# Hybrid encoder block on one core: the second MLP product's right operands on VectorE beside the first product, and three edges in the queues

## The chip, the cores and the metric

One core of a Trainium2 chip runs one layer of a streaming encoder (2048 positions, width 1024, MLP width 4096, all float32). The metric is the device time of one execution in microseconds (us), as the median of several runs. A profile is one execution recorded by the hardware: each engine's instructions with their times. Engines are called as the profile calls them: PE (TensorE, matmuls; PEld its weight loads), DVE (VectorE), ACT (ScalarE), POOL (GpSimd) and SP (SyncE, which only issues DMAs). Each engine works through its own instructions in order.

## The reference, cut to what matters

```python
mod = silu(c) @ w_ada + b_ada           # shift1, scale1, gate1, shift2, scale2, gate2
h = rms_norm(x, g_pre_mix) * (1 + scale1) + shift1
xin, b_gate, c_gate, q, k, v, g = split(h @ w_in)
y_conv = b_gate * causal_depthwise_conv3(c_gate * xin)
y_ret  = silu(g) * per_head_rms(retention(rotary(q), rotary(k), v))
x = x + gate1 * rms_norm(concat(y_conv, y_ret) @ w_out, g_post_mix)
h = rms_norm(x, g_pre_mlp) * (1 + scale2) + shift2
f = square(relu(h @ w_fc1)) @ w_fc2
x = x + gate2 * rms_norm(f, g_post_mlp)
```

## The kernel before, in words

**Precision.** Each float32 operand is split into a high part (an ACT cast to fp32r, `whi`, `wh`, `qh`, `fh`) and a low part (a DVE subtraction, `wlo`, `wl`, `ql`, `fl`). A product takes three matmuls: high by high, high by low, low by high (`mm3`, L142 to L144).

**The mixer** is a loop over four blocks `b` of 512 positions. Each block projects v, k, g, q, xin, the conv gate and the output gate in turn, does retention in four tiles, then the output product and a residual. Weights stream through three buffers (`wgroup`: load `raw` L134, cast L136, low part L138). `rotary` turns q and k out of PSUM with DVE (L541, L550) and a POOL add. `mod2` forms one modulation vector with eight DVE operations of 128x1024 (L429, L431), each on its own load `ada`; it is traced after the g projection in blocks 0 to 2, and once more in block 0.

**The MLP** works on two blocks `B` of 1024 positions, and each of its two products is done by a fast scheme with seven products of half size in place of eight (numbered 1 to 7; operands are sums and differences of quadrants). `fc1(B)` loops over 16 steps `t` of the MLP width. In each it makes sums of the weight quadrants on POOL (L901 to L904), does seven products `prod(i)` in the order 1, 2, 6, 7, 5, 3, 4 (at `t` = 0 of the first block, 4 comes before 7), squares, and stores the seven left operands of the second product to DRAM (`fd`). One product is 12 matmuls of 128x512. `fc2(B)` then runs seven products over 16 steps, each step loading a left operand (`fd`) and a right operand.

**The right operands of the second product.** Products 1, 2 and 3 use quadrants of the weight `w2` as they are. Those of 5, 7, 6 and 4 are differences, made once by `w2_prep(t)` for the 16 `t`: two loads of 512 KB (`w2r`), four POOL subtractions (L513), four stores to `w2d` (L515). `w2_some(n)` does `n` of them at set places of the mixer.

**The left operands** of block 0 (`h_left`) are split as 28 pieces before `fc1(0)`; three groups of four (for products 7, 5 and 3) are parked in DRAM (`sd`) and split during `t` = 0, where `left` is run to its end.

**Work beside fc1.** `fc1` takes a generator `beside` and calls `next` on it between products (`step`). For `fc1(0)` it is `mixer_end`: the residual of the mixer's last block (DVE L750, POOL L753, ACT squares L754) and then `h2_prep`, which transposes that block on PE (L492) for the second MLP block. For `fc1(1)` it is the tail of `fc2(0)`.

**Buffers.** The tag `x` has three buffers of 128x1024, shared by `x_tile`'s users: mod loads `ada`, residual loads `x`, `w2r` and, in fc2, `fw`. Weight halves `wh` and `wl` have three each, tag `r` ten; the `g` PSUM banks are six. `q(n, tag)` takes a 128x512 buffer from one of two pools by the parity of `n`.

**Order.** The program is traced in the order of the code, and a planner puts each engine's instructions in order from the traced order, the dependences and its own model of durations. So an instruction may go ahead of one that was traced earlier. `with tc.issue_after(ins)` adds an edge: what is traced inside on the engine of `ins` stays behind `ins` in that engine's order. It makes no engine wait on another.

Of the kernel before, what the change touches and what calls it, by code (L numbers as in the profile page):

```python
# [11 lines left out]
F32 = mybir.dt.float32  # L12
# [3 lines left out]
ALU = mybir.AluOpType  # L16
# [38 lines left out]
def block_kernel(  # L55
# [29 lines left out]
    def x_tile(name):  # L85
        return late.tile([P, D], F32, tag="x", name=nm(name), bufs=3)
# [417 lines left out]
    NP = DFF // P // 2  # L504
    w2d = {i: [dram.tile([P, 512], F32, name=f"w2d{i}_{t}") for t in range(NP)] for i in (5, 6, 7, 4)}

    def w2_prep(t):
        halves = [x_tile("w2r") for _ in range(2)]
        for i, c in enumerate(halves):
            nc.sync.dma_start(c, w2[t][:, i * 1024 : i * 1024 + 1024])  # L510
        c11, c12, c21, c22 = (c[:, i : i + 512] for c in halves for i in (0, 512))
        for o, a, b_ in ((c11, c12, c11), (c12, c22, c12), (c22, c22, c11), (c21, c21, c22)):
            nc.gpsimd.tensor_tensor(o, a, b_, op=ALU.subtract)  # L513
        for i, a in ((5, c11), (7, c12), (6, c22), (4, c21)):
            nc.sync.dma_start(w2d[i][t], a)  # L515

    w2_todo = iter(range(NP))

    def w2_some(n):
        for _, t in zip(range(n), w2_todo):  # L520
            w2_prep(t)

# [1 line left out]
    with pa_stack:  # L526
# [11 lines left out]
        def rotary(ps, coss, sins, t, dst):  # L538
            pv = ps.rearrange("p (h s d) -> p h s d", h=H, s=2)
            qa = tmp()  # L540
            nc.vector.tensor_tensor(  # L541
                qa.rearrange("p (x d) -> p x d", d=HALF),
                ps.rearrange("p (x d) -> p x d", d=HALF),
                coss[:, t, :].unsqueeze(1).to_broadcast([P, 2 * H, HALF]),
                op=ALU.mult,
            )
            qb = tmp()
            qbv = qb.rearrange("p (h s d) -> p h s d", h=H, s=2)
            for s in range(2):
                nc.vector.tensor_tensor(  # L550
                    qbv[:, :, s, :], pv[:, :, 1 - s, :],
                    sins[:, t, s, :].unsqueeze(1).to_broadcast([P, H, HALF]),
                    op=ALU.mult,
                )
            nc.gpsimd.tensor_tensor(dst, qa, qb, op=ALU.add)

        for b in range(NB):

# [5 lines left out]
            for ps in vps:  # L564
                v_ = at("va")
                nc.scalar.copy(v_, ps)
                vs.append(v_)
            if b > 0:
                w2_some(2)
            coss, sins = rope_tables(b)  # L570
            kds = []

            def k_end(t, ps):
                kr = tmp()
                rotary(ps, coss, sins, t, kr)
                kd = at("vb")
                nc.gpsimd.tensor_tensor(
                    kd.rearrange("p (h d) -> p h d", h=H),
                    kr.rearrange("p (h d) -> p h d", h=H),
                    kdec.unsqueeze(2).to_broadcast([P, H, DH]),  # L580
                    op=ALU.mult,
                )
                kds.append(kd)

            if b == 0:
                for t in range(3):
                    k_end(t, kps[t])
                k_end(3, gemm_nat(w_in(KK), h_cur, KS, ALL[3:])[0])
            else:
                for t, ps in enumerate(gemm_nat(w_in(KK), h_cur, KS)):  # L590
                    k_end(t, ps)

            sgs = []
            for ps in gemm_nat(w_in(GG), h_cur, KS):
# [1 line left out]
                nc.scalar.activation(sg, ps, AF.Silu)  # L596
                sgs.append(sg)
            if b < 3:
                part = mod2((0, 2, 3)[b])
            kTs = []  # L600
            for t in range(NT):
                tps = mbank()
# [102 lines left out]
            if b > 0:  # L705
                for _ in h2_prep(b - 1, h2_load(b - 1)):
                    pass
            w2_some(2 if b > 0 else 1)
            for j, ps in enumerate(gemm_t(w_in(BG), h_cur)):
                y = tmp()  # L710
                nc.vector.tensor_tensor(y, ps, cc[j], op=ALU.mult)
# [11 lines left out]
            for ch, tag in enumerate(("kT", "sg")):  # L723
                ms = []
                for t, ps in enumerate(gemm_nat([wout[ch * 4 + k0 // 2] for k0, _ in ko], ys, ko)):
                    m = at(tag)
                    nc.scalar.copy(m, ps)
                    nc.scalar.activation(junk(), m, AF.Square, accum_out=ssm[:, t, ch : ch + 1])
                    ms.append(m)
                mixs.append(ms)  # L730
                if ch == 0:
                    if b < NB - 1:
                        w2_some(1)

                    if b + 1 < NB:
                        rb = spread(r1)
                        h_cur = [h1_tile(b + 1, k, rb) for k in range(NK)]
# [77 lines left out]
    def split512(src, tile_of):  # L815
        hi, lo = tile_of("h"), tile_of("l")
        nc.scalar.copy(hi, src)  # L817
        nc.vector.tensor_tensor(lo, src, hi.bitcast(F32), op=SUB)  # L818
        return hi, lo

    def w_(part):
        return h_("w" + part)
# [62 lines left out]
    def fc1(B, hl, first, left=None, beside=None):  # L885
        def relu2(c, src):
            nc.scalar.activation(c, src, AF.Relu)
            nc.scalar.activation(c, c, AF.Square)

        def step(n=1):  # L890
            for _ in range(n if beside is not None else 0):
                next(beside, None)

        for t in range(NP):
            b11, b12, b21, b22 = first if t == 0 else quads(t)
            right = {}

            def prod(i):
                if i == 6:
                    t2 = r_()  # L900
                    nc.gpsimd.tensor_tensor(b11, b12, b11, op=SUB)  # L901
                    nc.gpsimd.tensor_tensor(t2, b22, b11, op=SUB)
                    nc.gpsimd.tensor_tensor(b12, b22, b12, op=SUB)
                    nc.gpsimd.tensor_tensor(b21, b21, t2, op=SUB)  # L904
                    right[6] = t2
                src = {1: b11, 2: b21, 7: b12, 5: b11, 3: b22, 4: b21}.get(i)
                hi, lo = split512(right[6] if i == 6 else src, w_)
                ps = bank()
                for p in range(4):
                    c = slice(p * P, p * P + P)  # L910
                    xh, xl = hl[i][p]
                    mm3(ps, hi[:, c], lo[:, c], xh, xl, p == 0, p == 3)
                return ps

            if t == 1 and left is not None:

                f12, f11, f21 = q(0, "junk"), q(0, "junk"), q(0, "sg")
            else:
                f12, f11, f21 = q(t, "kT"), q(t, "kT"), q(t, "kT")
            nc.scalar.copy(f12, prod(1))  # L920
            step()
            add(f11, prod(2), f12)
            step()
            relu2(f11, f11)
            nc.sync.dma_start(fd[B][1][t], f11)
            add(f12, prod(6), f12)
            step()
            f22 = q(t, "kT")
            if t == 0 and left is not None:
                nc.scalar.copy(f21, prod(4))  # L930
                for _ in left:
                    pass
                add(f22, prod(7), f12)
                add(f21, f21, f22, nc.gpsimd)
                beside_ = beside
                next(beside_, None)
                ps = prod(5)
                add(f12, ps, f12)
                add(f22, ps, f22)
                next(beside_, None)  # L940
            else:
                add(f21, prod(7), f12)
                step()
                ps = prod(5)
                add(f12, ps, f12)
                add(f22, ps, f21)
                step()
            relu2(f22, f22)
            nc.sync.dma_start(fd[B][4][t], f22)
            add(f12, prod(3), f12)  # L950
            relu2(f12, f12)
            nc.sync.dma_start(fd[B][2][t], f12)
            if t > 0 or left is None:
                add(f21, prod(4), f21)
            relu2(f21, f21)
            if beside is not None:
                for _ in beside:
                    pass
                beside = None

            s3 = q(t, "sg")
            nc.vector.tensor_tensor(s3, f11, f21, op=SUB)
            nc.sync.dma_start(fd[B][7][t], s3)
            nc.vector.tensor_tensor(f21, f21, f22, op=ADD)
            nc.sync.dma_start(fd[B][5][t], f21)
            s2_ = q(t, "sg")
            nc.vector.tensor_tensor(s2_, f21, f11, op=SUB)
            nc.sync.dma_start(fd[B][6][t], s2_)
            s4 = q(t, "sg")
            nc.vector.tensor_tensor(s4, f12, s2_, op=SUB)  # L970
            nc.sync.dma_start(fd[B][3][t], s4)

# [121 lines left out]
    left = h_left(0, hl[0], nc.vector, lambda n: r_(), False)  # L1094
    for _ in range(LEFT):
        next(left)
    fc1(0, hl[0], quads(0), left, mixer_end())
    tail = fc2(0, h_left(1, hl[1], nc.vector, lambda n: q(1, "kT" if n < 4 else "sg"), True))
    fc1(1, hl[1], quads(0), None, tail)
    fc2(1)  # L1100
# [84 lines left out]
```

## Time and profile before

| | |
|---|---|
| median of 3 runs | 2220.07 us (2219.22 to 2229.08) |
| profiled execution | 2219.7 us; span of its instructions 2217.9 us |
| mean granted TensorE clock | 0.994 |
| DMA | 428.22 MB, mean 193 GB/s |
| first matmul of fc1(0) / fc2(0) | 959.50 us / 1284.95 us |
| w2r loads issued | 174.5 to 807.5 us |

Busy time of an engine is the union of its instructions' times. Matmuls overlap in the pipeline, so each shows 0.39 us while the next starts after less; the distance of starts is what counts. "Idle before, releaser" names what the instruction had waited for last. A wait on an engine that is not the bound costs nothing by itself.

### The profile page before, as it was taken

Reading aid. Unit: us, or ns where it says so; the run is one execution under the profiler, and the core shown is the slowest. Engines: PE = TensorE matmul, PEld = TensorE weight load, DVE = VectorE, ACT = ScalarE, POOL = GpSimd, SP = SyncE. Lnnn points to the kernel's source line nnn. Section 1 sums busy time; section 2 is a strip of 40 time slices with the busy share of each in tenths; the row PEclk is TensorE's granted clock in tenths of the full one; section 3 lists DMA queues with packets and bytes.
Section 4 is the critical chain, followed back from the end, with each engine's and each line's share of the span. In section 5 each row is a group of like instructions: output and inputs, shape, how many; then the busy total and the mean of one; then the engine's idle time right before and its main releaser. Section 6 shows DMA issues by size and latency. Waiting matters only on the chain.

```text
span 2217.9 us, 28512 instructions
## 1 busy us (share of the span) xinstructions
PE 2143.4 (97%) x9784; PEld 1770.0 (80%) x9784; DVE 1435.4 (65%) x2186; ACT 995.5 (45%) x1730; POOL 559.2 (25%) x426
## 2 busy tenths in 40 slices
PE   6999999999999999989999999999999999999997
PEld 5787877877877888868888888888888888888885
DVE  8656863765577544776666787556766666555566
ACT  4423523253234422565555555445455555454453
POOL 0215164205332452152333301001333333010012
PEclk9999999999999999999999999999999999999998
DMA  8456477446555563665444376666764443666656
GB/s 342 133 172 224 139 261 240 147 156 228 190 199 188 189 234 97 231 204 196 157 157 157 129 250 215 200 191 190 273 210 157 157 156 123 209 191 195 196 189 251
DMA packets 197426, 428.22 MB, mean 193 GB/s; under 512 B 22561, under 2 KB 22561, under 8 KB 197281
## 3 DMA queue, kind: packets, MB, share of 16 engines
q1 hardware_dynamic: 197280, 426.41, 58.0%
q8 instruction: 76, 1.25, 0.2%
q14 instruction: 70, 0.57, 0.1%
HBM read 322.51 MB, written 103.81 MB: 192 GB/s over the span
## 4 chain that ended last, share of the span: by engine, by line
PE 70%; issue 11%; DMA 9%; DVE 4%; POOL 4%; ACT 1%; SPq 1%; DVEq 0%; POOLq 0%; ACTq 0%
PE g L142 20%; PE g L144 20%; PE g L143 20%; DMA w2r<-in_w 2%; PE m L142 2%; PE m L143 2%; PE m L144 2%; POOL w2r L513 2%; DMA w2d<-w2r 2%; DMA x<-in_x 1%; DMA ada<-in_ada 1%; DMA q<-h2d 1%; DVE wl L818 1%; DVE ql L818 1%; POOL sg L753 1%
## 5 line engine op out<-in xcount | busy, mean ns | idle before, releaser
L143 PE MATMUL g<-ql,wh 128*128 128x512 f32 x896 | 350.3, 391 | 8.7 <-DVE ql L818 8.7
L142 PE MATMUL g<-qh,wh 128*128 128x512 f32 x896 | 349.9, 391 | 1.4 <-ACT wh L817 1.1
L144 PE MATMUL g<-qh,wl 128*128 128x512 f32 x896 | 350.2, 391 | 0.1
L136 ACT CAST whi<-raw 128x1024 fp32r<-128x1024 f32 x148 | 155.6, 1052 | 338.7 <-PE g L144 186.0
L138 DVE TENSOR_TENSOR wlo<-raw,whi 128x1024 fp32r<-128x1024 f32 x148 | 200.5, 1360 | 159.0 <-ACT whi L136 157.9
L883 DVE TENSOR_TENSOR q<-g,q 128x512 f32<-128x512 f32 x267 | 178.4, 687 | 174.6 <-PE g L144 174.5
L143 PE MATMUL g<-wl,fh 128*128 128x512 f32 x680 | 264.9, 390 | 0.0
L144 PE MATMUL g<-wh,fl 128*128 128x512 f32 x680 | 264.6, 389 | 0.0
L818 DVE TENSOR_TENSOR fl<-fw,fh 128x512 fp32r<-128x512 f32 x218 | 161.4, 741 | 153.0 <-ACT fh L817 149.9
L817 ACT CAST wh<-r 128x512 fp32r<-128x512 f32 x224 | 138.9, 621 | 216.4 <-PE g L143 193.4
L817 ACT CAST fh<-fw 128x512 fp32r<-128x512 f32 x218 | 135.4, 621 | 214.9 <-DMA fw<-fd 201.3
L142 PE MATMUL g<-wh,fh 128*128 128x512 f32 x680 | 218.4, 389 | 0.9 <-ACT wh L817 0.9
L143 PEld LDWEIGHTS g<-ql,wh 128*128 128x128 f32 x896 | 168.9, 188 | 45.1 <-DVE ql L818 10.1
L142 PEld LDWEIGHTS g<-qh,wh 128*128 128x128 f32 x896 | 168.8, 188 | 37.4 <-ACT wh L817 1.8
L144 PEld LDWEIGHTS g<-qh,wl 128*128 128x128 f32 x896 | 168.9, 188 | 36.1 <-DVE wl L818 1.5
L818 DVE TENSOR_TENSOR wl<-fw,wh 128x512 fp32r<-128x512 f32 x218 | 156.6, 719 | 51.6 <-ACT wh L817 51.3
L1016 POOL TENSOR_TENSOR q<-q,gg 128x512 f32<-128x512 f32 x28 | 43.8, 1588 | 530.9 <-ACT q L1013 281.1
L818 DVE TENSOR_TENSOR wl<-r,wh 128x512 fp32r<-128x512 f32 x224 | 166.3, 743 | 9.8 <-ACT wh L817 9.5
L817 ACT CAST wh<-fw 128x512 fp32r<-128x512 f32 x218 | 135.2, 620 | 73.8 <-PE g L144 33.9
L901 POOL TENSOR_TENSOR r<-r,r 128x512 f32<-128x512 f32 x32 | 41.7, 1304 | 430.3 <-DVE wl L818 382.5
L142 PEld LDWEIGHTS g<-wh,fh 128*128 128x128 f32 x680 | 127.5, 188 | 28.2 <-ACT wh L817 1.7
L143 PEld LDWEIGHTS g<-wl,fh 128*128 128x128 f32 x680 | 127.7, 188 | 27.7 <-DVE wl L818 1.2
(258 smaller groups left out, 4412.5 us busy)
## 6 DMA issues: line engine op xcount, KB each, us to landing
raw<-in_win SPq DMA_DIRECT2D x116, 512.0 KB, 4.2
fd<-q SPq DMA_DIRECT2D x224, 256.0 KB, 2.2
fw<-fd SPq DMA_DIRECT2D x224, 256.0 KB, 2.7
r<-in_w SPq DMA_DIRECT2D x128, 256.0 KB, 4.7
fw<-w2d SPq DMA_DIRECT2D x128, 256.0 KB, 3.0
ada<-in_ada SPq DMA_DIRECT2D x48, 512.0 KB, 4.9
fw<-in_w SPq DMA_DIRECT2D x96, 256.0 KB, 3.5
w2r<-in_w SPq DMA_DIRECT2D x32, 512.0 KB, 5.0
```

The source lines that it names most:

```text
L136: nc.scalar.copy(hi, raw)
L138: (eng or nc.vector).tensor_tensor(lo, raw, hi.bitcast(F32), op=ALU.subtract)
L142: nc.tensor.matmul(ps, ah, bh, start=first, stop=False)
L143: nc.tensor.matmul(ps, ah, bl, start=False, stop=False)
L144: nc.tensor.matmul(ps, al, bh, start=False, stop=last)
L513: nc.gpsimd.tensor_tensor(o, a, b_, op=ALU.subtract)
L753: nc.gpsimd.tensor_tensor(m, m, xt[:, s], op=ALU.add)
L817: nc.scalar.copy(hi, src)
L818: nc.vector.tensor_tensor(lo, src, hi.bitcast(F32), op=SUB)
L883: (eng or nc.vector).tensor_tensor(o, a, b_, op=ADD)
L901: nc.gpsimd.tensor_tensor(b11, b12, b11, op=SUB)
L1016: eng.tensor_tensor(c, c, gg[1][:, j * 512 : j * 512 + 512], op=ALU.mult)
```

## The change

Four edits. The `w2_some` calls leave the mixer; `w2_prep` becomes a generator that does one subtraction on VectorE and its store per `next`, loads the next `t`'s halves two steps ahead, and is advanced once a `step` in `fc1(0)` from `t` = 3 on (13 x 5 calls for 64 subtractions); what is left runs after it. `mod2` in blocks 0 to 2 is traced inside `issue_after` of k's last rotary operation on DVE. The work beside `fc1` is traced inside `issue_after` of the latest low-part subtraction (`on_vector`), in both `fc1` calls; in `fc1(0)` it begins at `t` = 1 and is finished by the end of `t` = 2, where it began in `t` = 0 and ended there. And `t` = 1 of `fc1(0)` takes its `q` buffers from the pool that even `t` use (`u`).

```diff
-    def w2_prep(t):
-        halves = [x_tile("w2r") for _ in range(2)]
...
-            nc.gpsimd.tensor_tensor(o, a, b_, op=ALU.subtract)
-        for i, a in ((5, c11), (7, c12), (6, c22), (4, c21)):
-            nc.sync.dma_start(w2d[i][t], a)
+    def w2_prep():
+        def load(t, i):
+            c = x_tile("w2r")
             nc.sync.dma_start(c, w2[t][:, i * 1024 : i * 1024 + 1024])
+            return c
+        upper, lower = load(0, 0), load(0, 1)
+        for t in range(NP):
+            c11, c12, c21, c22 = (c[:, i : i + 512] for c in (upper, lower) for i in (0, 512))
+            for i, o, a, b_ in ((5, c11, c12, c11), (7, c12, c22, c12), (6, c22, c22, c11), (4, c21, c21, c22)):
+                nc.vector.tensor_tensor(o, a, b_, op=ALU.subtract)
+                nc.sync.dma_start(w2d[i][t], o)
+                if t + 1 < NP:
+                    if i == 7:
+                        upper = load(t + 1, 0)
+                    elif i == 4:
+                        lower = load(t + 1, 1)
+                yield
...
-            if b > 0:
-                w2_some(2)
...
             if b < 3:
-                part = mod2((0, 2, 3)[b])
+                with tc.issue_after(k_last.ins):
+                    part = mod2((0, 2, 3)[b])
...
-            w2_some(2 if b > 0 else 1)
...
-                    if b < NB - 1:
-                        w2_some(1)
...
-        nc.vector.tensor_tensor(lo, src, hi.bitcast(F32), op=SUB)
+        on_vector[0] = nc.vector.tensor_tensor(lo, src, hi.bitcast(F32), op=SUB)
...
         def step(n=1):
-            for _ in range(n if beside is not None else 0):
-                next(beside, None)
+            if left is not None and t > 2:
+                next(w2_todo, None)
+            for _ in range(n if beside is not None and (left is None or t > 0) else 0):
+                with tc.issue_after(on_vector[0].ins):
+                    next(beside, None)
...
+            u = 0 if t == 1 and left is not None else t
...
-            f22 = q(t, "kT")
+            f22 = q(u, "kT")
...
-                beside_ = beside
-                next(beside_, None)
                 ps = prod(5)
...
-                next(beside_, None)
...
-            if beside is not None:
-                for _ in beside:
-                    pass
+            if beside is not None and (left is None or t == 2):
+                with tc.issue_after(on_vector[0].ins):
+                    for _ in beside:
+                        pass
                 beside = None
-            s3 = q(t, "sg")
+            s3 = q(u, "sg")
...
+    w2_todo = w2_prep()
     fc1(0, hl[0], quads(0), left, mixer_end())
+    for _ in w2_todo:
+        pass
```

More of the change, by code (lines that the diff above doesn't have):

```diff
@@ L505, in block_kernel @@
     w2d = {i: [dram.tile([P, 512], F32, name=f"w2d{i}_{t}") for t in range(NP)] for i in (5, 6, 7, 4)}
-    def w2_prep(t):
-        halves = [x_tile("w2r") for _ in range(2)]
-        for i, c in enumerate(halves):
+    def w2_prep():
+        def load(t, i):
+            c = x_tile("w2r")
             nc.sync.dma_start(c, w2[t][:, i * 1024 : i * 1024 + 1024])
-        c11, c12, c21, c22 = (c[:, i : i + 512] for c in halves for i in (0, 512))
-        for o, a, b_ in ((c11, c12, c11), (c12, c22, c12), (c22, c22, c11), (c21, c21, c22)):
-            nc.gpsimd.tensor_tensor(o, a, b_, op=ALU.subtract)
-        for i, a in ((5, c11), (7, c12), (6, c22), (4, c21)):
[L515 to L521, printed above, removed]
+            return c
[11 more added lines that the diff above has]
+                yield
     with pa_stack:
@@ L549, in rotary @@
             for s in range(2):
-                nc.vector.tensor_tensor(
+                ins = nc.vector.tensor_tensor(
                     qbv[:, :, s, :], pv[:, :, 1 - s, :],
@@ L555, in rotary @@
             nc.gpsimd.tensor_tensor(dst, qa, qb, op=ALU.add)
+            return ins
         for b in range(NB):
@@ L574, in k_end @@
                 kr = tmp()
-                rotary(ps, coss, sins, t, kr)
+                k_last = rotary(ps, coss, sins, t, kr)
                 kd = at("vb")
@@ L583, in k_end @@
                 kds.append(kd)
+                return k_last
             if b == 0:
@@ L587, in block_kernel @@
                     k_end(t, kps[t])
-                k_end(3, gemm_nat(w_in(KK), h_cur, KS, ALL[3:])[0])
+                k_last = k_end(3, gemm_nat(w_in(KK), h_cur, KS, ALL[3:])[0])
             else:
                 for t, ps in enumerate(gemm_nat(w_in(KK), h_cur, KS)):
-                    k_end(t, ps)
+                    k_last = k_end(t, ps)
             sgs = []
@@ L817, in split512 @@
         nc.scalar.copy(hi, src)
-        nc.vector.tensor_tensor(lo, src, hi.bitcast(F32), op=SUB)
+        on_vector[0] = nc.vector.tensor_tensor(lo, src, hi.bitcast(F32), op=SUB)
         return hi, lo
+    on_vector = [None]
     def w_(part):
@@ L965, in fc1 @@
             nc.sync.dma_start(fd[B][5][t], f21)
-            s2_ = q(t, "sg")
+            s2_ = q(u, "sg")
             nc.vector.tensor_tensor(s2_, f21, f11, op=SUB)
             nc.sync.dma_start(fd[B][6][t], s2_)
-            s4 = q(t, "sg")
+            s4 = q(u, "sg")
             nc.vector.tensor_tensor(s4, f12, s2_, op=SUB)
```

## The prediction

> **What bounds the kernel now.** I read the page's first lines, then TensorE's waits, then busy time stretch by stretch, and last the timelines of the three places where TensorE stands. The page's span and busy line:
>
> ```profile
> span 2217.9 us, 28512 instructions
> PE 2143.4 (97%) x9784; PEld 1770.0 (80%) x9784; DVE 1435.4 (65%) x2186; ACT 995.5 (45%) x1730; POOL 559.2 (25%) x426
> ```
>
> TensorE is the bound: 74.5 us of the span without a matmul is the most that rearranging can reach, apart from matmuls at a lower clock. Busy time by stretch (columns: busy time and count for PE, weight load, DVE, ACT, POOL; then granted clock, DMA share, GB/s):
>
> ```profile
> 959.50:979.50 20.00, 11.86 (x49) 9.28 (x48) 17.33 (x19) 15.71 (x37) 12.84 (x8) 0.87 0.63 198
> 979.50:999.50 20.00, 17.23 (x60) 11.28 (x59) 16.97 (x30) 13.55 (x26) 10.96 (x10) 0.87 0.81 261
> ...
> 1039.50:1284.70 245.20, 245.20 (x1083) 203.05 (x1082) 161.34 (x235) 126.67 (x209) 74.17 (x49) 1.00 0.44 147
> ...
> 1589.00:1893.00 304.00, 304.00 (x1343) 251.81 (x1342) 207.96 (x305) 156.17 (x262) 103.70 (x72) 1.00 0.48 161
> ```
>
> 1343 matmuls in 304.00 us is a pitch of 0.2264 us; nothing in this change alters it. In the first two rows only 109 instructions ran in 40 us, where the pitch has room for 176. This is the opening of the first MLP product of block 0. Its ends, its transposes, its worst wait and what VectorE did meanwhile (timelines: start, duration, engine, line; in brackets the idle time and what ended it):
>
> ```profile
> 959.50 0.39 PE L142 MATMUL g<-qh,wh 128*128 128x512 f32 x1
> ...
> 970.41 0.50 PE L142 MATMUL g<-qh,wh 128*128 128x512 f32 x1 [0.54 <-ACT wh L817]
> 978.51 0.80 PE L143 MATMUL g<-ql,wh 128*128 128x512 f32 x1 [7.60 <-DVE ql L818]
> 979.10 0.63 PE L144 MATMUL g<-qh,wl 128*128 128x512 f32 x1
> 979.53 0.63 PE L142 MATMUL g<-qh,wh 128*128 128x512 f32 x1
> ...
> 1001.60 0.60 PE L492 MATMUL m<-ident,kT 128*128 128x128 f32 x4
> 1001.96 0.47 PE L142 MATMUL g<-qh,wh 128*128 128x512 f32 x1
> ```
>
> ```profile
> 1284.95 1.07 PE L142 MATMUL g<-wh,fh 128*128 128x512 f32 x4
> ```
>
> ```profile
> 967.54 1.19 DVE L750 SCALAR_TENSOR_TENSOR kT<-kT,rmr,gg 128x512 f32<-128x512 f32 x1
> 968.65 1.78 DVE L750 SCALAR_TENSOR_TENSOR sg<-sg,rmr,gg 128x512 f32<-128x512 f32 x1
> ...
> 975.04 3.41 DVE L818 TENSOR_TENSOR ql<-r,qh 128x512 fp32r<-128x512 f32 x2
> ```
>
> ```profile
> 968.14 1.74 POOL L753 TENSOR_TENSOR sg<-sg,x 128x512 f32<-128x512 f32 x1
> ```
>
> Product 7 waits 7.6 us for the low parts of its left operand; VectorE was doing the last residual (L750) ahead of them, at 1.78 us an operation instead of 0.74 while POOL added beside it. When TensorE resumes, the clock is down: 979.10 to 979.53 is 0.43 us a matmul, against 0.2264. Whole stage: 1284.95 - 959.50 = 325.45 us for 7 x 16 x 12 = 1344 matmuls (304.3 us) and 32 transposes (0.09 us each by 1001.60 to 1001.96, 2.9 us). **18.3 us is lost here**, nearly all before 1000.
>
> The mixer, before 959, loses more but in small pieces. Its waits (from 140 to 960 us: total, times, longest):
>
> ```profile
> PE g L142 <- DVE tmp L550: 3.7, 2, 2.1
> PE g L142 <- ACT whi L136: 3.3, 2, 3.0
> PE g L144 <- DVE yl L701: 2.8, 2, 1.5
> PE m L492 <- ACT tmp L496: 2.4, 6, 0.4
> PE g L143 <- DVE wlo L138: 2.3, 3, 1.5
> PE m L655 <- DVE sg L666: 2.3, 1, 2.3
> ```
>
> **The change, part by part.** The profiled execution took 2219.7 us (span 2217.9 and 1.8 around it), 0.4 below the median of 2220.07; the sum is made against 2219.7.
>
> *(a) The last residual starts at t = 1 instead of t = 0, and its VectorE work, like the MLP tail's beside fc1(1), stands behind the newest weight split.* Nothing is removed: 8 L750, 8 POOL adds, 16 squares on ACT, 4 loads, 8 stores and the 32 transposes move some 19 us later (84 matmuls an iteration by the pitch). At t = 0 VectorE then meets the low parts of products 7, 5 and 3 directly: up to 16 of them and 7 weight splits, 8 sums and 4 differences, 35 operations at 0.69 to 0.74, about 24 us against 19 us of TensorE, with a head start of some 6 us in which VectorE now idles. So t = 0 still loses up to 3 us. At t = 1 and 2 the residual meets a running pipeline: 18 operations of fc1 an iteration (12.5 us, from 161.34 us over 12.9 iterations) and 9 to 14 us of L750. If every POOL add (8 x 1.74 = 13.9 us) pairs with one VectorE operation, as at 968, VectorE needs 26 us in that iteration, 7 us too many, less the 5.4 us that three weight buffers let it lead. I take 3 us for t = 0 and 3.5 us for t = 1 and 2, so **-11.8 us** of the 18.3; the ends are -6 (all pairings, and the clock dropping again) and -17. The `q` buffers that t = 1 now takes from the other pool are reused an iteration later, after a store of 2 to 3 us: nothing, covered by 19 us. The fc1(1) edge costs nothing: that row above has no idle TensorE to lose or win.
>
> *(b) mod products behind k's last rotary.* VectorE's timeline in blocks 1 and 2:
>
> ```profile
> 315.40 0.75 DVE L429 TENSOR_SCALAR wide<-ada,sc 128x1024 f32<-128x1024 f32 x1 [6.48 <-DMA ada<-in_ada]
> 316.07 0.69 DVE L541 TENSOR_TENSOR tmp<-g,coss 128x512 f32<-128x512 f32 x1
> ...
> 552.37 0.75 DVE L429 TENSOR_SCALAR wide<-ada,sc 128x1024 f32<-128x1024 f32 x1 [5.97 <-DMA ada<-in_ada]
> ```
>
> The first mod product blocks VectorE until its load lands; k's rotary stands behind it and TensorE behind the rotary's bank. With the edge the rotary goes first, and the L550 row loses its 3.7 us. The mod products then run some 6 us later; their result is wanted after the q and xin products, tens of us on, so their delay costs nothing unless the same blocking falls on a weight split instead (the far end, 0). **-3.7 us.**
>
> *(c) Leaving the mixer: 64 POOL subtractions, 32 loads of 512 KB, 64 stores of 256 KB.* The subtractions and their transfers (one group of the line, the tile's landing times, and SyncE's queue around 360):
>
> ```profile
> L513 POOL TENSOR_TENSOR w2r<-w2r x32: 1272/1292/2214, 179.5 to 815.1; 128x512 f32<-128x512 f32 x32
> ```
>
> ```profile
> DMA to landing us min/median/max: 2.0/3.7/7.1
> ```
>
> ```profile
> 355.49 5.06 SPq L515 DMA_DIRECT2D w2d<-w2r  x2
> 360.64 0.38 SPq L134 DMA_DIRECT2D raw<-in_win  x1
> ...
> 363.57 0.38 SPq L134 DMA_DIRECT2D raw<-in_win  x1
> 368.45 5.58 SPq L245 DMA_DIRECT2D x<-in_x  x3
> ```
>
> 64 x 1.29 = 83 us leave POOL, which is off the path (25%). What counts is SyncE's queue: at 355 it stands 5 us in stores that wait for POOL, and the weight loads behind them come late; the whi wait of 3.3 us, and part of the wlo wait, follow. The three `x` buffers are then free for the mod and x loads. I credit the whi row and half of wlo (4.5 us) and about a third of the 7.5 us in yl, sg and L496 (2.5 us), which have other causes too: **-7 us**. Ends: 0 (another load takes the place in the queue) and -14 (these rows, and the clock dips with them).
>
> *(d) The 64 differences on VectorE from t = 3 of fc1(0).* VectorE there, by group:
>
> ```profile
> L818 DVE TENSOR_TENSOR wl<-r,wh 128x512 fp32r<-128x512 f32 x88 | 63.2, 718 | 0.1
> L883 DVE TENSOR_TENSOR q<-g,q 128x512 f32<-128x512 f32 x90 | 60.9, 689 | 75.8 <-PE g L144 75.8
> L962 DVE TENSOR_TENSOR q<-q,q 128x512 f32<-128x512 f32 x13 | 14.8, 1137 | 6.4 <-ACT q L888 6.4
> ```
>
> The same form costs 0.69 to 0.72, 1.14 when it meets POOL; at 0.8 it is 51 us. VectorE has 245.2 - 161.3 = 83.9 us idle there, 75.8 of it waiting for TensorE's products: the cover. It goes to 86% busy; with the cover gone every further us is a us of TensorE. Ends for this term: 0, and with all 64 at 1.75, 112 - 84 = +28. Each difference waits for a load, and behind it on VectorE stand weight splits and bank releases. A lower half is loaded two steps (two products, 5.4 us) ahead, the upper one more; landing is 3.7 us at the median of loads and stores together. SyncE gets 96 more issues; w1's loads run an iteration ahead, so a store waiting on VectorE there delays nothing wanted within 19 us. DMA: 33.6 MB over 245 us is 137 GB/s on top of 147; the share goes to about 0.85, just above the 0.81 row. Last, the three `x` buffers hold these halves until t = 15, so fc2(0)'s first operands are loaded in the last 8 to 11 us of fc1(0), not far ahead: 0 to 3 us. I take **+2 us** in all.
>
> Sum: -11.8 - 3.7 - 7 + 2 = -20.5; 2219.7 - 20.5 = 2199.2, or **2200 us** by the median.
>
> One rule speaks against the move. The Trainium skill, "Perfetto Trace Analysis", Optimizing Scalar/DVE Operations, says work may be handed to GpSimd when VectorE is saturated, and that the two share a read port, so handing over may bring nothing; here work goes the other way, to an engine at 66%. It would come out worse only with VectorE full, which the slower rival below prices.
>
> **The rivals.**
>
> *R1, the gain shrinks to the opening (2211 us).* POOL's adds and the fc1 operations slow each other through t = 1 and 2: (a) gives only -6; (c) gives -1 because the x and mod loads take the queue's places; (b) -3.7, (d) +2: -8.7. For it: 1.78 us at 968 beside POOL's 1.74. Against: at 967 to 973 VectorE had nothing else to interleave, while beside a running fc1 two residual operations come a step. By the Trainium skill, "SBUF — State Buffer", Who interferes with whom, a VectorE instruction with two SBUF inputs and a GpSimd one that reads SBUF exclude each other; the 1.78 agrees, and by that rule alone every POOL add costs one stretched operation, which is this case.
>
> *R2, VectorE becomes the bound of fc1(0) (2253 us).* One mechanism: a difference at the head of VectorE's queue while its half is still landing. Were the 16 lower halves to land at 7.1 us (1.7 late, 27 us) and operations to stretch to 1.75 (112 us), 139 - 84 = 55 us would come through: 2200 - 2 + 55. It decides from 84 us on, 1.3 us a difference with its wait; slower by 0.5% needs about 1.8. Against: POOL is busy only 30% of that stretch, and 0.72 is the mean of 88 like operations there.
>
> *R3, nothing shows (2220 us).* The order of instructions comes from a planner, and moving this much work changes it everywhere; new small waits in the mixer and at fc2(0)'s start eat (b) and (c), and t = 1 repeats t = 0's stall.
>
> **How the numbers follow.** Forecast (2184 to 2208): 0.61. R1 (2207 to 2215): 0.19. R3: 0.08. R2: 0.12. Low end: (a) -17, (b) -3.7, (c) -14, (d) 0 gives 2185; with the doubt on each I say 2184. The high end is 2220, leaving out R2 and half of R3; the forecast's own range is 2184 to 2208. About 0.5%, 11 us, is what a measurement of this kernel can tell from no change: faster than 2209 holds the forecast and a quarter of R1, 0.66; same 0.22; slower 0.12.
>
> **What would show it.** (a): the product-7 wait of 7.6 us and the clock of 0.87 are gone, fc1(0) takes about 315 us, L750 stands at 980 to 1000. (b): no wait on L550 in blocks 1 and 2. (c): no w2r operation in the mixer, the whi waits shrink. (d): L513's successor at 0.7 to 0.9 us, VectorE at 85% in t 3 to 15, TensorE still without gaps, fw loads near fc1(0)'s end. It is wrong if TensorE waits on wl in t 3 to 15 (R2), if t = 1 and 2 lose over 10 us (R1), or if the mixer's length before the first MLP matmul stays at 959.

## The result and the profile after

The change makes the kernel 0.9% faster: the median is 2203.97 us (2198.31 to 2206.85, six runs) against 2221.93 us for the kernel before beside it, ratio 0.9912 (95% interval 0.9898 to 0.9926). The profiled execution took 2202.43 us. Its span and busy line:

```profile
span 2200.4 us, 28427 instructions
PE 2139.1 (97%) x9784; PEld 1767.9 (80%) x9784; DVE 1472.7 (67%) x2250; ACT 988.8 (45%) x1730; POOL 469.2 (21%) x362
```

64 operations moved from POOL (426 to 362) to VectorE (2186 to 2250); TensorE has 61.3 us of the span without a matmul instead of 74.5. Where the 17.5 us of span came from is read from the first matmul of each stage in TensorE's timeline (start, duration, engine, line):

```profile
935.83 0.39 PE L142 MATMUL g<-qh,wh 128*128 128x512 f32 x1
...
1263.74 0.39 PE L142 MATMUL g<-wh,fh 128*128 128x512 f32 x1
```

| profiled execution | mixer ends | fc1(0) | fc2(0) | fc1(1) | fc2(1) |
|---|---|---|---|---|---|
| before | 959.50 | 325.45 | 306.95 | 304.64 | 305.4 |
| after | 935.83 | 327.91 | 308.56 | 304.69 | 307.5 |

The mixer gained 23.7 us, more than the whole change; fc1(0), in which the residual should have given 11.8 and the differences cost 2, is 2.5 us longer; the rest gave back 3.8. In the mixer the gain can be split by the stretch as a whole (columns as in the prediction; one row of each kernel, before and then after):

```profile
140.00:959.50 819.50, 793.94 (x3840) 658.32 (x3840) 509.83 (x793) 298.14 (x536) 267.89 (x213) 1.00 0.58 193
```

```profile
140.00:935.83 795.83, 786.59 (x3834) 655.50 (x3834) 497.81 (x793) 297.39 (x535) 178.95 (x149) 1.00 0.47 156
```

TensorE's gaps fell from 819.50 - 793.94 = 25.6 us to 9.2, and its busy time for nearly the same matmuls by another 7.4 us. Part of the 7.4 is the clock: in stretches of 10 us the granted clock is 0.95 and 0.88 from 310 to 330 and 0.83 from 380 to 390 before, some 3.4 us together, and 1.00 throughout after; six more records before are another 1.4 us by the pitch; the rest isn't shown. What is left of its waits there:

```profile
PE m L492 <- ACT tmp L496: 2.4, 6, 0.4
PE g L143 <- DVE wlo L138: 2.3, 3, 1.5
...
PE g L142 <- DVE tmp L555: 0.4, 1, 0.4
```

The waits on whi and yl are gone, and that on k's rotary (L555, the old L550) went from 3.7 to 0.4 us. The opening of fc1(0), 60 us in thirds:

```profile
935.83:955.83 20.00, 18.88 (x83) 15.31 (x82) 17.34 (x28) 17.76 (x36) 4.09 (x3) 1.00 0.74 237
955.83:975.83 20.00, 15.34 (x58) 11.55 (x57) 20.00 (x22) 11.71 (x27) 16.48 (x12) 0.91 0.59 190
975.83:995.83 20.00, 19.03 (x88) 15.43 (x87) 19.89 (x30) 14.15 (x29) 10.97 (x9) 1.00 0.94 335
```

Instead of 49 and 60 matmuls in the first 40 us, 83 and 58 ran. The second row is where the residual now stands: VectorE busy all 20.00 us, POOL 16.48 us, TensorE short of 30 matmuls. VectorE and then POOL in it (timelines):

```profile
953.42 1.75 DVE L753 SCALAR_TENSOR_TENSOR kT<-kT,rmr,gg 128x512 f32<-128x512 f32 x1
955.09 1.78 DVE L753 SCALAR_TENSOR_TENSOR sg<-sg,rmr,gg 128x512 f32<-128x512 f32 x1
...
972.25 0.74 DVE L753 SCALAR_TENSOR_TENSOR kT<-kT,rmr,gg 128x512 f32<-128x512 f32 x1
```

```profile
957.99 1.74 POOL L756 TENSOR_TENSOR sg<-sg,x 128x512 f32<-128x512 f32 x1
...
970.04 1.74 POOL L756 TENSOR_TENSOR sg<-sg,x 128x512 f32<-128x512 f32 x1
```

Alone the operation takes 0.74 us, beside a POOL operation of 128x512 1.75 to 1.78, on both sides of the change. The Trainium skill, "SBUF — State Buffer", Who interferes with whom, states that the port pair which VectorE and GpSimd share is held as an exclusive lock; these durations agree.

The loss that was not expected lies further on, beside the differences. One stretch of before, then three of after:

```profile
1060.00:1120.00 60.00, 60.00 (x267) 49.67 (x266) 39.57 (x59) 30.37 (x50) 18.22 (x12) 1.00 0.47 158
```

```profile
1060.00:1120.00 60.00, 56.47 (x245) 45.23 (x244) 49.42 (x73) 27.14 (x47) 17.65 (x12) 1.00 0.91 312
1120.00:1180.00 60.00, 57.35 (x246) 46.71 (x245) 51.23 (x75) 26.87 (x47) 18.50 (x12) 0.97 0.94 325
1180.00:1250.00 70.00, 70.00 (x311) 57.95 (x310) 48.56 (x70) 38.28 (x64) 24.74 (x16) 1.00 0.47 163
```

In 1060 to 1180, 491 matmuls ran where 533 fit: 42 at 0.2264 us are 9.5 us. VectorE is at 82 to 85% there, not full. The DMA share, 0.99 from 1000 to 1040, is 0.91 to 0.94 here, then 0.47: the differences' transfers were crowded into the first part. The tile's answer after:

```profile
L519 DVE TENSOR_TENSOR w2r<-w2r x32: 674/680/1784, 982.0 to 1176.8; 128x512 f32<-128x512 f32 x32
...
  DMA w2r<-in_w: 16.3, 11
...
DMA to landing us min/median/max: 2.0/5.1/7.5
```

64 differences ran from 982.0 to 1176.8, one in 3.0 us. The code calls for five in a `t` of 19 us, one in 3.8 us, and for the first at `t` = 3, which begins some 65 us after 935.83 (57 by the pitch and the 36 matmuls, 8 us, that the three rows above are short of). VectorE stood idle 16.3 us, in 11 stops, at their heads for loads; one of these from its timeline with the weight split behind it, the matmul that waited for that split, and what TensorE waited for from 1000 us to fc1(0)'s end:

```profile
1081.43 1.42 DVE L519 TENSOR_TENSOR w2r<-w2r,w2r 128x512 f32<-128x512 f32 x2 [3.22 <-DMA w2r<-in_w]
...
1084.56 0.68 DVE L821 TENSOR_TENSOR wl<-r,wh 128x512 fp32r<-128x512 f32 x1
```

```profile
1085.30 0.50 PE L144 MATMUL g<-qh,wl 128*128 128x512 f32 x1 [0.95 <-DVE wl L821]
```

```profile
PE g L144 <- DVE wl L821: 6.2, 6, 2.4
```

Before each of the six waits VectorE's order has differences ahead of the split; four of the six come within 6 us after a stop of VectorE for a load. The busy DMA engines did not make the weights themselves late: from 1000 to 1250 us ScalarE's weight casts waited for no load, and for POOL's sums 4.2 us, where the paced kernel e7 below has 7.6 and loses nothing.

### The profile page after: what moved, and what is told of

Same layout as the page of the kernel before. It is cut to its first block, busy times and chain, and to the rows that moved or that the text cites. A ratio compares the mean times of both kernels' runs of the same rounds, so it can differ in the third digit from the quotient of the medians.

```text
span 2200.4 us, 28427 instructions
## 1 busy us (share of the span) xinstructions
PE 2139.1 (97%) x9784; PEld 1767.9 (80%) x9784; DVE 1472.7 (67%) x2250; ACT 988.8 (45%) x1730; POOL 469.2 (21%) x362
## 4 chain that ended last, share of the span: by engine, by line
PE 57%; DMA 6%; DVE 4%; issue 4%; ACT 1%; POOL 0%; SPq 0%; DVEq 0%; POOLq 0%
PE g L144 17%; PE g L142 17%; PE g L143 17%; PE m L142 2%; PE m L144 2%; PE m L143 2%; DMA fw<-fd 2%; DMA w2r<-in_w 1%; DMA w2d<-w2r 1%; DVE wl L821 1%; DMA fw<-w2d 1%; DVE q L888 1%; DVE w2r L519 0%; DVE sg L753 0%; ACT qh L820 0%
## 5 line engine op out<-in xcount | busy, mean ns | idle before, releaser
L138 DVE TENSOR_TENSOR wlo<-raw,whi 128x1024 fp32r<-128x1024 f32 x148 | 194.9, 1321 | 168.1 <-ACT whi L136 167.5
L821 DVE TENSOR_TENSOR wl<-r,wh 128x512 fp32r<-128x512 f32 x224 | 171.6, 766 | 10.5 <-ACT wh L820 10.0
L144 PEld LDWEIGHTS g<-wh,fl 128*128 128x128 f32 x680 | 127.6, 188 | 26.3
```

The costliest lines, as they stand in the source:

```text
L138: (eng or nc.vector).tensor_tensor(lo, raw, hi.bitcast(F32), op=ALU.subtract)
L144: nc.tensor.matmul(ps, al, bh, start=False, stop=last)
L821: on_vector[0] = nc.vector.tensor_tensor(lo, src, hi.bitcast(F32), op=SUB)
```

## The experiments

Three questions. Which part gave the mixer's 23.7 us? What did the residual and the differences each do to fc1(0)? And why did the differences cost more than 2 us? On the last: either VectorE's load is too high (51 us of work and POOL's stretching, theory L), or the differences run in bunches, ahead of their places, so that their loads come late and weight splits stand behind them (theory Q). Ratios are to the kernel before on the same chip (medians of 2222 to 2224 us), with 95% intervals.

**One part at a time.** The edge on `mod2` alone, onto the kernel before:

```diff
             if b < 3:
-                part = mod2((0, 2, 3)[b])
+                with tc.issue_after(k_last.ins):
+                    part = mod2((0, 2, 3)[b])
```

> Before, with the edge of the mod products behind k's last rotary alone. After starts its MLP 23.7 us earlier than before (first MLP matmul at 935.83 against 959.50), twice what the prediction gave to the edge and to w2's leaving together. Theory A (w2's transfers and POOL work in the mixer cost most of it, the edge only the two waits on L550): the first MLP matmul comes 3 to 5 us earlier, about 955.5, and the time falls by about 4 us. Theory B (the edge itself reorders VectorE and gives most): 12 us or more earlier.

Measured: 0.9969 (0.9956 to 0.9983), 2218.14 us; mixer to 954.63, fc1(0) 323.59. TensorE's wait on k's rotary is gone.

The differences' move alone (generator, VectorE, `t > 2`):

```diff
-            if b > 0:
-                w2_some(2)
...
+            if left is not None and t > 2:
+                next(w2_todo, None)
```

> Before, with the right operands moved to VectorE in fc1(0) alone; mod products and last residual as before. Theory A: the mixer ends 17 to 20 us earlier (first MLP matmul near 941), fc1(0) keeps its opening loss of 18 us and pays about 11 us for the 64 differences (stage about 336 us against 325.45), net about -9 us. Theory B: the mixer ends at most 10 us earlier, net 0.

Measured: 0.9945 (0.9925 to 0.9965), 2211.94 us. Its stage starts:

```profile
940.38 0.39 PE L142 MATMUL g<-qh,wh 128*128 128x512 f32 x1
...
1273.82 0.39 PE L142 MATMUL g<-wh,fh 128*128 128x512 f32 x1
```

The mixer is 19.1 us shorter than before, fc1(0) with 333.44 us 8.0 longer: most of the mixer's gain and all of fc1(0)'s loss are this part's. TensorE's wait on k's rotary is almost gone here too, though this kernel lacks the edge (waits from 140 to 940 us):

```profile
PE g L142 <- DVE tmp L555: 0.3, 1, 0.3
```

The residual's move alone:

```diff
-            for _ in range(n if beside is not None else 0):
-                next(beside, None)
+            for _ in range(n if beside is not None and (left is None or t > 0) else 0):
+                with tc.issue_after(on_vector[0].ins):
+                    next(beside, None)
```

> Before, with the last residual moved to t = 1 and 2 and queued behind the weight splits alone; the right operands stay in the mixer. Theory A (the residual's move gains about 9 us and the 64 differences ate it): fc1(0) takes 315 to 318 us against 325.45, the mixer is as before, net about -8 us. Theory C (the residual's move gains nothing, its cost only moves to t = 1 and 2): fc1(0) stays at 323 to 327, net 0 to -2 us.

Measured: 0.9965 (0.9951 to 0.9978), 2216.57 us. Its stage starts:

```profile
954.21 0.39 PE L142 MATMUL g<-qh,wh 128*128 128x512 f32 x1
...
1272.89 0.39 PE L142 MATMUL g<-wh,fh 128*128 128x512 f32 x1
```

fc1(0) takes 318.68 us, 6.8 less than before. Its mixer has every engine's instructions in the same order as before's, and yet ends 5.3 us earlier: so much a single profile's mixer differs with the order unchanged. e1's 4.9 us therefore can't be told from this by the profile; by the run times e1's gain is 4 to 10 us.

The change without the differences (no loads, operations or stores; products 4 to 7 of the second product read plain quadrants):

```diff
-            if left is not None and t > 2:
-                next(w2_todo, None)
...
-            j = {1: 0, 2: 2, 3: 3}.get(i)
+            j = {1: 0, 2: 2, 3: 3, 4: 1, 5: 0, 6: 2, 7: 3}.get(i)
```

> After, with the right operands' work left out altogether (no w2r loads, no differences, no stores; fc2 reads quadrants of w2 for all seven products, so the same number of loads). It prices that work inside fc1(0). Theory A: the mixer as in after (first MLP matmul at 936), fc1(0) 315 to 317 us against after's 327.91, net 11 to 13 us under after, about 2191 us. Theory C: fc1(0) 324 or more, within 3 us of after.

Measured: 0.9864 (0.9845 to 0.9884), 2195.69 us; mixer to 939.94, fc1(0) 316.81. Against the change's 327.91 the differences cost 11.1 us there; by the run times 0.9912 - 0.9864, 11 us. Residual alone: 325.45 - 316.81 = 8.6 us gained. The stage itself varies: in the five kernels here that open fc1(0) as before does (before, e1, e5, e6, e10) it takes 323.06 to 325.48 us, so the residual's gain lies between 4 and 9 us.

**The cost of the differences.** The change with an edge on each, so that it stays behind the newest weight split:

```diff
             if left is not None and t > 2:
-                next(w2_todo, None)
+                with tc.issue_after(on_vector[0].ins):
+                    next(w2_todo, None)
```

> After, with each step of the right operands also traced behind the latest weight split on VectorE. In after the planner ran the 64 differences ahead in bunches, 982 to 1177 us, with DMA at 0.99 and VectorE waiting for w2r loads; they cost fc1(0) 11 us against none at all. Theory Q (the bunching is the cost: a difference waits at the head of VectorE's queue for a load that is not there yet): spread over 1000 to 1255 they cost 0 to 3 us, fc1(0) 317 to 320 us, net 8 to 11 us under after, about 2194. Theory L (VectorE's load is the cost, 64 operations however placed): fc1(0) stays at 325 to 330, within 3 us of after.

Measured: 0.9861 (0.9836 to 0.9886), 2193.61 us. Stage starts, three stretches, and the tile:

```profile
937.44 0.39 PE L142 MATMUL g<-qh,wh 128*128 128x512 f32 x1
...
1254.31 0.39 PE L142 MATMUL g<-wh,fh 128*128 128x512 f32 x1
```

```profile
1060.00:1120.00 60.00, 60.00 (x266) 49.67 (x266) 53.85 (x74) 31.53 (x53) 22.30 (x14) 1.00 0.84 282
1120.00:1180.00 60.00, 60.00 (x267) 49.67 (x266) 54.08 (x72) 30.76 (x51) 23.01 (x15) 1.00 0.87 288
1180.00:1250.00 70.00, 70.00 (x310) 57.96 (x309) 62.00 (x85) 34.47 (x59) 21.77 (x13) 1.00 0.85 285
```

```profile
L519 DVE TENSOR_TENSOR w2r<-w2r x32: 682/685/1784, 1001.5 to 1241.8; 128x512 f32<-128x512 f32 x32
...
DMA to landing us min/median/max: 2.0/5.2/7.5
```

VectorE is busier than in the change (89 to 90% against 82 to 85%), and TensorE has no gap: fc1(0) takes 316.87 us, with 64 differences, against 316.81 without any. From 1000 us to the end of the stage no wait of TensorE is listed, and the tile's answer lists no idle time of VectorE before a difference. So L falls and Q stands. Landing is the same (5.1 and 5.2 us at the median, 7.5 at most); what differs is the pace. One difference in 3.75 us gives a lower half, loaded two steps ahead, 7.5 us, the slowest landing; at 3.0 us and in pairs it had 6 or less.

fc2(0) now takes 312.76 us, 4 to 6 more than in the kernels above, as its first operands wait for the `x` buffers that the last differences hold (e11 bears this out). Two more versions: the lower half loaded one difference earlier, to see whether a late half still holds VectorE in fc1(0), and, on top of it, the differences from `t` = 2, so that the buffers come free sooner.

```diff
-                    elif i == 4:
+                    elif i == 6:
```

> The kernel before it (e7), with the lower half of the next step loaded one difference earlier (behind 6 in place of 4). If a late lower half still holds VectorE in e7, this takes 1 to 3 us more off; if the spreading alone cured it, the two are the same within 2 us.

Measured: 0.9854 (0.9833 to 0.9876), 2190.49 us; fc1(0) 317.04, fc2(0) 311.04. fc1(0) is as in e7 within 0.2 us: no late half was left to mend there.

```diff
-            if left is not None and t > 2:
+            if left is not None and t > 1:
```

> The kernel e8 with the differences beginning at t = 2 of fc1(0) in place of t = 3, so that they end at t = 14. In e7 and e8 fc2(0) takes 312.8 and 311.0 us where it takes 307.2 with no such work; its first operands find the x buffers late. Expected: fc2(0) back at 307 to 308.5, against 0 to 3 us more in t = 2, where h2_prep runs too: net 0 to 4 us under e8, about 2189. If t = 2 has no room, fc1(0) goes over 320 and nothing is gained.

Measured: 0.9865 (0.9845 to 0.9885), 2192.98 us; fc1(0) 317.23, fc2(0) 308.23. fc2(0) is mended, as expected; the further 0 to 4 us of the whole time don't show, as it can't be told from e8's. Of the versions of the whole kernel these three are the fastest, 10 to 13 us under the change by their ratios.

**The mixer.** The kernel before without the subtractions on POOL (loads and stores stay), without the stores (`w2d`; products read plain quadrants), and with the loads alone:

```diff
-        for o, a, b_ in ((c11, c12, c11), (c12, c22, c12), (c22, c22, c11), (c21, c21, c22)):
-            nc.gpsimd.tensor_tensor(o, a, b_, op=ALU.subtract)
```

> Before, with the 64 POOL subtractions left out of the mixer; loads and stores of w2r stay, so w2d holds raw quadrants. Taking all of w2 out of the mixer brought the first MLP matmul from 954 to 959 down to 936 to 940 us. Theory P (POOL: its port shared with VectorE, and stores in SyncE's queue waiting for it): most of it comes back, start at 941 to 946. Theory T (the transfers: bytes, SyncE's places, the three x buffers): start at 950 or later.

Measured: 0.9966 (0.9954 to 0.9979), 2217.90 us; mixer to 956.08, 3.4 us earlier than before's and inside the spread of 5.3.

```diff
-        for i, a in ((5, c11), (7, c12), (6, c22), (4, c21)):
-            nc.sync.dma_start(w2d[i][t], a)
```

> Before, with the 64 stores to w2d left out of the mixer; loads and POOL subtractions stay (fc2 reads quadrants of w2 itself). Theory S (stores at the head of SyncE's queue wait for POOL and hold the weight loads, and the x buffers wait for them to land): most comes back, start at 941 to 946. Theory P's other half (VectorE slowed beside POOL): start at 952 or later.

Measured: 1.0022 (1.0008 to 1.0037), 2227.02 us; mixer to 959.91. Taking 64 stores off the queue gains nothing; by the interval it costs 2 to 8 us.

> Before, with only the 32 loads of w2r left in the mixer (no subtractions, no stores; fc2 reads quadrants of w2). Leaving out the subtractions or the stores alone brought the first MLP matmul nowhere (956.08 and 959.91 against 954 to 959.5); leaving out all of w2 brought 936 to 940. Theory H (the x buffers: one of the three is gg0's until the last residual, so w2's two halves take both that are left, and mod and x loads wait until the halves are done with): the loads alone still take both, but only for some 5 us each: start at 944 to 952. Theory T (bytes and SyncE's places): half the bytes are gone, start at 946 to 950. If it is 954 or later, the mere presence of the loads among the x buffers' users is enough, whatever is done with them.

This one leaves out both. Measured: 0.9977 (0.9965 to 0.9990), 2217.68 us; mixer to 954.23. The loads alone keep most of the loss, as the last case of the expectation has it.

Then the opposite: the change without the differences, but with 64 copies of 256 KB from DRAM to DRAM at the old places in the mixer, which use SyncE's queue and the DMA engines and no buffer:

```diff
+            for i, j in ((5, 0), (7, 1), (6, 3), (4, 2)):
+                with tc.issue_after(on_sp[0].ins):
+                    nc.sync.dma_start(w2d[i][t], w2[t][:, j * 512 : j * 512 + 512])
```

> After without the right operands' work (e4), with 64 copies of 256 KB from w2 to w2d within DRAM at the places where the mixer had w2, each queued on SyncE behind the latest weight load; w2d holds raw quadrants. Adds the transfers and SyncE's places without x buffers and POOL. Theory T: the first MLP matmul falls back from 940 to 950 or later. Theory H: it stays at 936 to 943, within 4 us of e4.

Measured: 0.9861 (0.9844 to 0.9879), 2191.84 us; mixer to 936.53, at a DMA share of 0.54. So bytes, and 64 more places in the queue behind weight loads, cost nothing that shows.

Last, the change without the differences, and one of the three `x` buffers held through the mixer:

```diff
+    held_x = x_tile("held")
+    nc.gpsimd.memset(held_x, 0.0)
```

> After without the right operands' work (e4), with one more x buffer held through the mixer by a tile that is written once and read at its end; mod and x loads then go through one buffer in place of two. No transfer and no POOL work is added. Theory H: the first MLP matmul falls back from 940 to 950 or later, about 10 us slower than e4 (2196). Theory T: it stays at 936 to 943.

Measured: 0.9906 (0.9885 to 0.9927), 2200.72 us; mixer to 941.18, fc1(0) 320.31. Against e4 it is slower by 5 us in the medians and 9 in the ratios, but its mixer ends only 1.2 us later, where theory H had 950 or later. One buffer less does not by itself bring the loss back.

So the kernels fall into two groups by one feature. With w2r loads in the mixer it ends at 959.50, 954.63, 954.21, 956.08, 959.91 and 954.23; without (e12 apart) at 935.83, 940.38, 939.94, 937.44, 935.37, 937.59 and 936.53. The means are 956.4 and 937.6, 18.8 us apart, with no overlap. The mod edge differs between the groups too: of the first only e1 has it, of the second only e2 lacks it. Like against like, the w2r loads are worth 16.4 us without the edge (956.8 against e2's 940.38) and 17.5 with it (e1's 954.63 against 937.1), and the edge 2 to 3 us. What the loads do to SyncE's queue, in its waits from 140 to 950 us, before:

```profile
SPq L134 <- DVE wlo L138: 214.0, 70, 8.1
SPq L515 <- POOL w2r L513: 92.9, 57, 6.0
SPq L515 <- DMA w2r<-in_w: 26.8, 11, 4.2
...
SPq L510 <- DMA w2d<-w2r: 20.0, 11, 5.0
SPq L746 <- DMA w2d<-w2r: 14.9, 6, 4.3
...
SPq L245 <- DMA w2d<-w2r: 10.0, 6, 4.4
...
SPq L427 <- DMA w2d<-w2r: 7.6, 4, 3.5
```

with the loads alone (e10), and after (to 930 us):

```profile
SPq L134 <- DVE wlo L138: 282.9, 83, 8.2
SPq L510 <- DMA w2r<-in_w: 37.1, 16, 4.0
...
SPq L741 <- DMA w2r<-in_w: 16.3, 7, 4.8
...
SPq L245 <- DMA w2r<-in_w: 10.2, 5, 3.2
SPq L427 <- DMA w2r<-in_w: 8.4, 4, 2.7
```

```profile
SPq L134 <- DVE wlo L138: 369.0, 100, 8.2
```

The first row of each is harmless: SyncE stands at the next weight load, as far ahead as the buffers allow; it grows from 214.0 to 282.9 and 369.0. Before, the two L515 rows (119.7 us) are stores that stand at the head of the queue for their own data, a subtraction or a load. The others are time there for a buffer that an earlier w2r piece holds: 52.5 us before, 72.0 with the loads alone, none after. The mod and residual loads (L427, L245, L741 and L746) wait there too, for buffers that they share with w2r. TensorE in e10:

```profile
PE g L142 <- ACT whi L136: 4.0, 1, 4.0
PE g L143 <- DVE wlo L138: 3.9, 5, 1.6
```

So the w2r loads' presence costs the mixer some 16 to 18 us, which e2 and the groups show; by what path is open. The waits for buffers are a path that fits, but they don't set the loss: 52.5 us before, 115 in e6 and 72.0 in e10, where the mixers end at 959.50, 959.91 and 954.23, and e12 speaks against the number of buffers alone. e10's loads and e13's copies also differ in more than the buffers: in size, in writing to the core's own memory or to DRAM, and in the edge behind a weight load. w2r with buffers of its own in the mixer was not tried.

## Why the prediction came out right, step by step

2204 us is 4 from the forecast, but by terms that were off in opposite directions, so that its nearness is in good part luck: by the groups the mixer gave 8 us more than (b) and (c) together, (a) 3 to 5 less, and (d) cost 6 to 9 more. One of the prediction's own signs of being wrong came true: TensorE waits on `wl` from 1000 us on (6.2 us).

- **(a) the residual, -11.8 predicted: -6.8 to -8.6 (e3, e4).** Mechanism right: the 7.6 us wait for product 7 is gone, the residual's VectorE work stands 18 to 38 us after the first matmul. The size is nearer to R1's -6: of the 7 us that full pairing with POOL's adds puts on VectorE I let 3.5 through, and pairing was nearly full (eight VectorE operations from 953 to 979 took 1.75 to 1.78); the row from 955.83 alone is short of 30 matmuls, 6.8 us.
- **(b) the mod edge, -3.7: the row went from 3.7 to 0.4 us.** Alone it gives 4.9 us in the profile, beside a spread of 5.3, and 4 to 10 by the run times. But the row is at 0.3 us in e2 as well, which has no edge: either part removes this wait, so the terms (b) and (c) don't simply add, and beside (c) the edge is worth 2 to 3 us by the groups, within the spread.
- **(c) w2 out of the mixer, -7: about -16 to -19.** This is the term that failed, beyond its end of -14. (b) and (c) were to give 10.7 together, and the groups differ by 18.8. I summed single rows of TensorE's waits and credited a third or a half of them, though the gap of the whole stretch, 25.6 us, could be read. And the mechanism failed with the size: stores that wait for POOL are the largest row of w2r in SyncE's queue, but the kernel without stores is no faster. What e10 shows in its place is that the loads alone keep the loss; that they do it through the `x` buffers is not shown. I had counted three such buffers as free for others; the last residual's gate vector `gg` sits in one of them through the mixer, so w2r's pair had two to share with every mod and residual load.
- **(d) the differences on VectorE, +2: +8.0 (e2) to +11.1 (e4).** The operations cost what was said (0.68 us at the median; VectorE 82 to 85%). fc2(0) took 1.6 us more, but kernels without differences there (e3, e5, e6) take as much. What failed is the assumption of one difference a step: `next` sets the traced place only, and the planner ran them ahead of it. With the edge the term is 0.06 us in fc1(0), as the cover of 84 us says, and 4 to 6 us at fc2(0)'s start until the differences begin a `t` earlier (e11).

(d)'s lead was thin besides: 5.4 us stood against a landing of 3.7, the median of loads and stores together. Apart they are, before (KB each, median us from issue to landing):

```profile
w2r<-in_w SPq DMA_DIRECT2D x32, 512.0 KB, 5.0
...
w2d<-w2r SPq DMA_DIRECT2D x64, 256.0 KB, 2.3
```

R2's chain is what (d) met, a difference at the head of VectorE's queue waiting for its half, but at 16.3 us of VectorE's time and 9.5 of TensorE's, not 55; and not because VectorE was the bound. R1's slowing is in (a), its cancelling of (c) isn't; R3, no change, is out by the interval. On the rule of the Trainium skill that was weighed ("Perfetto Trace Analysis", Optimizing Scalar/DVE Operations, on handing work off a saturated VectorE): at 90% in e7, paced, VectorE cost TensorE nothing, so no run here reaches the case the rule is for.

## What to carry to other kernels

Work put beside a running product needs an edge that holds it at its place, not only a place in the code: the same 64 operations cost the product 11 us when an automatic order let them bunch, and nothing when each stayed behind the newest weight split. Side loads can cost far more than their bytes or their places in the queue, as the w2r loads did here; leave them out once to learn their price, and look at who shares their buffers, though that this was the path is not shown. When small waits are spread over a long stretch, take the stretch's whole gap as the bound, and compare groups of kernels by a feature, since one profile's stage moved by 5 us with the order unchanged.

## What the runs showed of the hardware that was not expected

64 copies of 256 KB from DRAM to DRAM beside the mixer's weight stream cost no time that shows (e13: mixer to 936.53 against 939.94 without them). Before and e3, with one order of instructions in the mixer, ended it at 959.50 and 954.21. The 5.3 us come together in steps of at most 1.4 us over the whole mixer, mostly at waits of TensorE; what makes these differ no row shows.
